# Hybrid attention trunk: the sums of weight blocks kept unit by unit in DRAM and moved as rows of 8 KB, and the last norm's sum and roots taken through TensorE and PSUM

## The chip, the core and the metric

The kernel runs on one core of one Trainium2 chip. The metric is the device time of one execution in microseconds (us); a kernel's figure is the median of its timed runs. A profile is one further execution with the hardware profiler on. Its engines are called PE (TensorE; PEld is its weight load), ACT (ScalarE), DVE (VectorE), POOL (GpSimd) and SP (SyncE, which here only issues DMAs).

## The reference

One layer of a streaming encoder in float32: 2,048 frames of 1,024 features, 16 heads of 64, chunked attention with a learned relative bias, then a SwiGLU block with 2,816 hidden features. Each sub-layer stands between two RMS norms.

```python
def rms_norm(x, g):
    y = x * lax.rsqrt(jnp.mean(x * x, axis=-1, keepdims=True) + RMS_EPS)
    return y * g

def reference(x, ...):
    h = rms_norm(x, g_pre_mix)
    m = chunk_relpos_attention(h, w_qkv, w_o, rel_bias)   # chunk c sees chunks c-8 .. c
    x = x + rms_norm(m, g_post_mix)
    h = rms_norm(x, g_pre_ffn)
    return x + rms_norm((silu(h @ w_gate) * (h @ w_up)) @ w_down, g_post_ffn)
```

## The kernel before, in words

**Layout and products.** Activations lie transposed, features on the 128 partitions and tokens along the free dimension, in blocks of 512 tokens (`HALF`); two blocks make a group, and there are two groups. Every dense product is done with float32 split in two parts (`split`, `split_part`: a rounded part by ACT, the rest by a DVE subtraction, L128/L129 for weights and L347/L348 for activations) and takes three matmuls (`products`, L192 to L194).

**Order of the work.** TensorE's order is written out by hand; the other engines' orders are chosen by the scheduler within the data's dependencies, and each engine then runs its own queue strictly in order. So an instruction that waits holds up all that stands behind it on its engine. Work that belongs beside the matmuls is put in a list (`later`) of steps with a cost; `tick` runs steps as matmuls are emitted, one tick for three matmuls of 512 columns, and `pause(w)` is an empty step of w ticks.

**Attention.** For each group 64 slots are run (16 jobs of a pair of heads, four blocks of 128 queries each). In a slot PE computes the scores (L555/L556), DVE adds the bias and finds the maximum (L564), ACT takes the exponentials and their sums (L568), DVE the reciprocals (L571), POOL scales the probabilities (L572, one per head), and PE transposes them (L588, and the fifth block at L599), from where DVE and ACT copy them to SBUF (L591, L593, L600). The slots are filled up with the dense products of the following jobs.

**The feed-forward block** uses a seven-product scheme for a two-by-two block product (Strassen's, in Winograd's form). Of the factors on the weights' side four are sums of weight blocks, S1 to S4: S1 = A21 + A22, S2 = A11 + S1, S3 = A11 + A21, S4 = A12 + S2, the differences being all on the activations' side. They are made once, beside the attention, for 11 gate/up units (128 x 1024 floats, 512 KB a block) and 11 down units (128 x 512 floats, 256 KB), in DRAM alone: `weight_sums` yields steps, of which one is run per slot (t from 5 to 51 in the first group, 0 to 51 in the second). A step holds DRAM-to-DRAM copies of a first term, issued from SP (`copy`, through the helper at L71), and accumulating DMAs of a second term, issued from POOL (`add`, L868). An add is put behind POOL's last softmax scaling (`issue_after`), so it stands in POOL's queue between the scalings of two slots. Units take turns, gate/up and down; unit u's four copies are in the steps 4u to 4u+3, its adds in 4u+5, 4u+6, 4u+8 and 4u+11. The program reserves 512 bytes of each SBUF partition for the descriptors of such DMAs (`dynamic_dma_scratch_size`). A sum is a tensor of 128 rows with the unit's index inside the row, so a block is moved as 128 pieces of 4 KB or 2 KB; the blocks of the down weights lie the same way. During the feed-forward block the factors are read back, `gate_up_stream` and `down_stream`, through SP.

**The end.** The last group's down product ends with the second half of its output columns for token block 0. That last product is done in two halves of 256 tokens; after each, `ended` puts the norm of that half on the list. `rstd_steps` adds the squares over the partitions by matmuls against a column of ones, one per 128 tokens (L258), takes mean and epsilon on DVE (L260), the power -1/2 on POOL (L262), and `spread` transposes the roots to rows on PE (L274) and copies them to SBUF by ACT (L275). The squares of each output tile are taken by ACT (L243) and added up by DVE (L244); the tile itself comes from PSUM through a DVE addition (L1075). `finish` multiplies the output by the roots (L1375), adds the residual (L1376), both on DVE, two tiles of 128 features a time for the first half and four for the second, and issues the store. The norm of the other token block (`Post.finish`) was done beside the product before; there half of the residual sums run on POOL (L392).

Of the kernel before, what the change touches and what calls it, by code (L numbers as in the profile page):

```python
# [9 lines left out]
F32 = mybir.dt.float32  # L10
F32R = mybir.dt.float32r
AF = mybir.ActivationFunctionType
ALU = mybir.AluOpType
# [3 lines left out]
P = 128  # L17
# [33 lines left out]
def trunk(  # L51
# [162 lines left out]
    def pause(w):  # L214
        return [(w, lambda: None)]
# [27 lines left out]
        act.activation(sq, src, AF.Square)  # L243
        eng.tensor_tensor(total, total, sq, op=ALU.add)  # L244

    def rstd_steps(total, dst, wait=8.0, keep=None, bank=None):

        nb = total.shape[-1] // P
        bank = bank or norm_bank
        r = {}

        def by_token():
            pt = bank("pssq")
            for b in range(nb):
                pe.matmul(pt[:, 0, b : b + 1], total[:, b * P : b * P + P], ones[:, 0:1], start=True, stop=True)  # L258
            m = const.tile([P, 4], F32, tag="ms", name="ms", bufs=2)
            dve.tensor_scalar(m[:, :nb], pt[:, 0, :nb], 1.0 / D, EPS, op0=ALU.mult, op1=ALU.add)  # L260
            r[0] = const.tile([P, 4], F32, tag="rs", name="rs", bufs=2) if keep is None else keep
            pool.tensor_tensor(r[0][:, :nb], m[:, :nb], neg_half.to_broadcast([P, nb]), op=ALU.pow)  # L262

        return [(1.0, by_token)] + pause(wait) + [(1.0, lambda: spread(r[0], dst, bank))]

    def norm_bank(name):
        return ps.tile([P, 4, P], F32, tag="mm", name=name)

    def spread(r, dst, bank=norm_bank):

        pt = bank("prs")
        nb = dst.shape[-1] // P
        for b in range(nb):
            pe.transpose(pt[:, b, :], r[:, b : b + 1].to_broadcast([P, P]), ident)  # L274
        act.activation(dst, pt[:, :nb, :].rearrange("p b t -> p (b t)"), AF.Copy)  # L275

    class Prep:

# [569 lines left out]
    NC = NF // 2  # L848

    def gate_up_at(c):  # L850
        return {n: w_gu[c, BLOCK_AT[n]] for n in BLOCK_AT}, {n: sum_gu[n][:, c, :] for n in sum_gu}

    def down_at(c):
        return {n: w_d[BLOCK_AT[n]][:, c, :] for n in BLOCK_AT}, {n: sum_d[n][:, c, :] for n in sum_d}

    units = [at(c) for c in range(NC) for at in (gate_up_at, down_at)]

    def weight_sums():

        def copy(to, a):
            with tc.issue_after(last_sp[0].ins):
                sp.dma_start(to, a)

        def add(to, a):
            with tc.issue_after(last_pool[0].ins):
                pool.dma_start(to, a, accum_op=ALU.add)  # L868
# [25 lines left out]
    def gate_up_stream(c, n):  # L894

        a = FACTOR[n]

        def load():
            raw = phase["fp"].tile([P, 1024], F32, tag="w4", name="raw4", bufs=4)
            sp.dma_start(raw, w_gu[c, BLOCK_AT[a]] if a in BLOCK_AT else sum_gu[a][:, c, :])  # L900
            return raw

        def make(raw):
            w = w_tile(f"gu{c}_{n}")
            split_part(*w, raw)
            return w

        return load, make, 4, 3

    def down_stream(g, n, c):  # L910

        a = FACTOR[n]

        def load():
            raw, cols = narrow("raw_d"), narrow("raw_a")
            src = w_d[BLOCK_AT[a]] if a in BLOCK_AT else sum_d[a]
            sp.dma_start(raw, src[:, c, :])
# [347 lines left out]
    def dense():  # L1265
# [59 lines left out]
        for g in range(NG):  # L1325
# [29 lines left out]
            total, begun = [], set()  # L1355
# [12 lines left out]
            def finish(here, per):  # L1368

                n = here.stop - here.start  # L1370
                r = total[0][:, here].rearrange("p (o t) -> p o t", o=1).to_broadcast([P, per, n])

                def one(k):
                    a, b_ = (v[:, k : k + per, here] for v in (y[0], res[0]))
                    dve.tensor_tensor(a, a, r, op=ALU.mult)  # L1375
                    dve.tensor_tensor(b_, b_, a, op=ALU.add)  # L1376
                    sp.dma_start(out[i][:, k : k + per, here], b_)

                return [(0.0, lambda k=k: one(k)) for k in range(0, KT, per)]

            def ended(n):
                if n == 0:
                    post = Post([y[1][:, dt, :] for dt in range(KT)], total[1], POST_FFN, res[1], out[i + 1])
                    later.extend(pause(4.0) + rstd_steps(post.total, post.total, 5.0) + post.finish(2.0, 2))
                    return
                drain()
                first, second = slice(0, N), slice(N, HALF)
                here = (first, second)[n - 1]
                later.extend(pause((1.0, 0.0)[n - 1]) + rstd_steps(total[0][:, here], total[0][:, here], 3.0))
                if n == 2:  # L1390
                    later.extend(finish(first, 2) + finish(second, 4))

            yield from down(g, keep, ended)
            drain()
# [100 lines left out]
def _layout(inputs):  # L1495
# [10 lines left out]
    for p in range(NPAIR):  # L1506
# [19 lines left out]
        "w_d": np.stack([wd[:, j::2, HALF * i : HALF * i + HALF] for i, j in ((0, 0), (1, 0), (1, 1), (0, 1))]),  # L1526
    }


# [18 lines left out]
```

## Time and profile before

| | |
|---|---|
| median of 3 runs | 2446.33 us |
| fastest, slowest of them | 2441.12, 2449.23 us |
| the profiled execution, its own time | 2441.91 us |
| its span, first to last instruction | 2440.1 us |
| mean granted TensorE clock | 0.996 of full |
| DMA | 488.41 MB, mean 200 GB/s |
| adds' queue (software) | 12,672 packets, 34.61 MB |

The profile is one execution. Its views are read so: the page gives busy times and shares per engine; the list of waits tells which group of instructions waited for which, with the total, the count and the longest; a timeline row has start, duration, engine, line, operation, tiles, shapes and count, with the idle time ahead of it and what ended that in brackets ("issue" is idle time that the profile explains by no semaphore); a windows row has a stretch, its length, the busy time and count of PE, PEld, DVE, ACT and POOL, the granted clock, the DMA engines' busy share and GB/s. Matmuls are pipelined: one of 512 columns is shown for 0.39 us, but they start 0.23 us apart.

### The profile page before, as it was taken

The page shows a single profiled execution, that of the slowest core. Times are in us where ns is not written, and L with a number is a line of the kernel's source. Part 1 is how long each engine was busy: PE and PEld are TensorE (multiplying, and loading weights), DVE is VectorE, ACT ScalarE, POOL GpSimd, SP SyncE. Part 2 cuts the span into 40 slices and gives each one's busy share as a digit, 9 for nine tenths or more (in the row PEclk, how much of TensorE's full clock was granted, in tenths as well). Part 3 has the DMA queues.
Part 4 walks back from the last instruction along what each step waited for, and adds up shares of the span by engine and source line. Part 5 has one row for each costly group of instructions (what it writes and reads, how often), then busy time and mean ns, then how long its engine had stood idle before and what let it go on. Part 6 is the DMA issues. An engine that isn't in the chain of part 4 may idle for free.

```text
span 2440.1 us, 34891 instructions
## 1 busy us (share of the span) xinstructions
PE 2399.6 (98%) x12554; PEld 1993.0 (82%) x12554; DVE 1468.8 (60%) x2569; ACT 1030.7 (42%) x1807; POOL 302.6 (12%) x379
## 2 busy tenths in 40 slices
PE   9999999999999999999999999999999999999997
PEld 8887878788888888878888788888888888888886
DVE  6555455767555554667566665577666655555577
ACT  5444334654344443545333333365443333334444
POOL 0233233201233332210000000000000000000001
PEclk9999999999999999999999999999999999999999
DMA  7689888757898975546476755377667655457654
GB/s 219 196 216 234 221 229 203 222 183 200 226 250 214 243 182 133 144 143 225 157 252 201 242 171 170 123 246 256 210 214 246 219 178 160 135 170 243 195 188 147
DMA packets 209884, 488.41 MB, mean 200 GB/s; under 512 B 25360, under 2 KB 27424, under 8 KB 208432
## 3 DMA queue, kind: packets, MB, share of 16 engines
q1 hardware_dynamic: 197040, 451.59, 58.3%
q0 software_dynamic: 12672, 34.61, 9.3%
q8 instruction: 99, 1.62, 0.3%
q14 instruction: 73, 0.60, 0.1%
HBM read 356.54 MB, written 148.42 MB: 207 GB/s over the span
## 4 chain that ended last, share of the span: by engine, by line
PE 48%; DMA 4%; DVE 3%; issue 1%; ACT 0%; SPq 0%; DVEq 0%; ACTq 0%
PE pd L192 6%; PE pd L193 6%; PE pd L194 6%; PE pb L192 4%; PE pb L193 4%; PE pb L194 4%; PE pa L192 3%; PE pa L193 3%; PE pa L194 3%; PE pc L192 3%; PE pc L194 3%; PE pc L193 3%; DMA b<-x 1%; DMA res<-in_x 1%; DMA y<-y 1%
## 5 line engine op out<-in xcount | busy, mean ns | idle before, releaser
L568 ACT ACTIVATE sc<-sc,nmax 128x640 f32<-128x640 f32 (+4 forms) x256 | 193.1, 756 | 277.5 <-DVE nmax L564 276.7
L192 PE MATMUL mm<-hb,whi 128*128 128x512 f32 x704 | 290.0, 412 | 0.5 <-ACT y L239 0.5
L194 PE MATMUL mm<-hb,wlo 128*128 128x512 f32 x704 | 277.0, 393 | 0.0
L193 PE MATMUL mm<-hb,whi 128*128 128x512 f32 x704 | 276.1, 392 | 0.0
L572 POOL TENSOR_SCALAR sc<-sc,rows 128x640 f32<-128x640 f32 (+4 forms) x256 | 198.6, 813 | 438.4 <-DVE rows L571 418.7
L564 DVE CUSTOM_DVE_ANT_0 sc<-st,bias 128x640 f32<-128x640 f32 (+4 forms) x256 | 179.6, 738 | 100.2 <-PE st L556 94.9
L192 PE MATMUL pb<-hb,whi_gu_T 128*128 128x512 f32 x528 | 206.9, 392 | 4.8 <-DVE terms L980 4.8
L194 PE MATMUL pb<-hb,wlo_gu_T 128*128 128x512 f32 x528 | 206.0, 390 | 0.0
L193 PE MATMUL pb<-hb,whi_gu_T 128*128 128x512 f32 x528 | 205.9, 390 | 0.0
L262 POOL TENSOR_TENSOR rs<-ms,neg_half 128x4 f32<-128x4 f32 (+1 forms) x11 | 16.7, 1520 | 1248.1 <-DVE ms L260 1248.1
L192 PEld LDWEIGHTS mm<-hb,whi 128*128 128x128 f32 x704 | 132.9, 189 | 35.2 <-issue 14.7
L194 PEld LDWEIGHTS mm<-hb,wlo 128*128 128x128 f32 x704 | 132.4, 188 | 29.4
L193 PEld LDWEIGHTS mm<-hb,whi 128*128 128x128 f32 x704 | 133.1, 189 | 19.4
L193 PE MATMUL pd<-a,whi_d_T 128*128 128x512 f32 (+1 forms) x368 | 139.9, 380 | 0.4 <-DVE a L348 0.4
L192 PE MATMUL pd<-a,whi_d_T 128*128 128x512 f32 (+1 forms) x368 | 140.0, 381 | 0.0
L194 PE MATMUL pd<-a,wlo_d_T 128*128 128x512 f32 (+1 forms) x368 | 139.7, 380 | 0.0
L192 PE MATMUL pa<-hb,whi_gu_B 128*128 128x512 f32 x352 | 137.7, 391 | 0.5 <-ACT terms L961 0.5
L193 PE MATMUL pa<-hb,whi_gu_B 128*128 128x512 f32 x352 | 137.0, 389 | 0.0
L194 PE MATMUL pa<-hb,wlo_gu_B 128*128 128x512 f32 x352 | 137.0, 389 | 0.0
L192 PE MATMUL mm<-whi,hb 128*128 128x256 f32 x448 | 133.5, 298 | 0.0
L555 PE MATMUL st<-k,q 128*128 128x384 f32 (+1 forms) x448 | 131.9, 315 | 0.2 <-DVE nmax L564 0.2
L129 DVE TENSOR_TENSOR wlo_gu_T<-raw,whi_gu_T 128x1024 fp32r<-128x1024 f32 x88 | 107.4, 1221 | 40.5 <-ACT whi_gu_T L128 40.3
(219 smaller groups left out, 5642.8 us busy)
## 6 DMA issues: line engine op xcount, KB each, us to landing
raw<-gu_S SPq DMA_DIRECT2D x88, 512.0 KB, 3.9
raw<-in_w_gu SPq DMA_DIRECT2D x66, 512.0 KB, 4.1
q<-stage SPq DMA_DIRECT2D x128, 256.0 KB, 5.8
y<-y SPq DMA_DIRECT2D x96, 256.0 KB, 3.8
gu_S<-in_w_gu SPq DMA_DIRECT2D x44, 512.0 KB, 7.6
raw_a<-aT SPq DMA_DIRECT2D x88, 256.0 KB, 3.6
raw_d<-d_S SPq DMA_DIRECT2D x88, 256.0 KB, 3.6
raw<-in_w_a SPq DMA_DIRECT2D x42, 512.0 KB, 6.3
```

The lines of the kernel that those rows point to most:

```text
L129: dve.tensor_tensor(lo, raw, hi.bitcast(F32), op=ALU.subtract)
L192: pe.matmul(pt, a_hi, b_hi, start=first, stop=False, skip_group_check=go_on)
L193: pe.matmul(pt, a_hi, b_lo, start=False, stop=False, skip_group_check=go_on)
L194: pe.matmul(pt, a_lo, b_hi, start=False, stop=last, skip_group_check=go_on)
L262: pool.tensor_tensor(r[0][:, :nb], m[:, :nb], neg_half.to_broadcast([P, nb]), op=ALU.pow)
L555: pe.matmul(st[:, a:b], q[:, 2 * h, cols], kk[:, h, key], start=True, stop=False)
L564: dve.tensor_tensor_reduce(out=sc[:, :n], in0=st[:, c0 : c0 + n], in1=rev, scale=-1.0, scalar=3.0e38, op0=ALU.add, op1=ALU.min, accum_out= ...
L568: act.activation(sc[:, :n], sc[:, :n], AF.Exp, bias=nmax, scale=-1.0, accum_out=rows[:, 0:1])
L572: last_pool[0] = pool.tensor_scalar(sc[:, :n], sc[:, :n], rows[:, 1:2], 1.0, op0=ALU.mult, op1=ALU.mult)
```

## The change

Two parts that touch each other nowhere.

*The sums.* Their tensors, and the down weights on the host, are laid out unit by unit, so that one unit's block is contiguous. Copies and adds see a block as 64 longer rows and are limited to 8 KB a row: 64 rows for a gate/up block, 32 for a down block. A pair of units (gate/up c and down c) now shares 8 steps: the four copies of the gate/up unit are in the steps 8c, 8c+2, 8c+4, 8c+6, its adds in 8c+4 (S1), 8c+8 (S2), 8c+10 (S3) and 8c+14 (S4), and the down unit does the same one step later. Each step so has one copy and one add, of a large and a small block by turns.

*The end.* The squares of token block 0's last feature tile stay apart; `rstd_steps` adds them by a second matmul per 128 tokens (`extra`). The roots' rows aren't copied to SBUF: `finish` reads them from PSUM (`then`), and the sums and roots use the banks "pd". `finish` takes two feature tiles a time in both halves; POOL adds the residual for the first two tiles of the first half and for the first four of the second, DVE for the rest, and `finish` of both halves is now one step, `end`. The other block's norm begins after a pause of 6 ticks, not 4.

```diff
-    sum_gu = {n: dram.tile([P, NF // 2, 1024], F32, name=f"gu_{n}") for n in ("S1", "S2", "S3", "S4")}
-    sum_d = {n: dram.tile([P, NF // 2, HALF], F32, name=f"d_{n}") for n in ("S1", "S2", "S3", "S4")}
+    sum_gu = {n: dram.tile([NF // 2, P, 1024], F32, name=f"gu_{n}") for n in ("S1", "S2", "S3", "S4")}
+    sum_d = {n: dram.tile([NF // 2, P, HALF], F32, name=f"d_{n}") for n in ("S1", "S2", "S3", "S4")}
...
             for b in range(nb):
-                pe.matmul(pt[:, 0, b : b + 1], total[:, b * P : b * P + P], ones[:, 0:1], start=True, stop=True)
+                terms = [total] if extra is None else [total, extra]
+                for n, t in enumerate(terms):
+                    pe.matmul(
+                        pt[:, 0, b : b + 1], t[:, b * P : b * P + P], ones[:, 0:1],
+                        start=n == 0, stop=n == len(terms) - 1,
+                    )
...
+        def back():
+            if then is None:
+                spread(r[0], dst, bank)
+            else:
+                then(transposed(r[0], nb, bank))
...
+        def long(t):
+            return t.rearrange("(a b) c -> a (b c)", b=2)
 
         def copy(to, a):
             with tc.issue_after(last_sp[0].ins):
-                sp.dma_start(to, a)
+                last_sp[0] = nc.sync.dma_start(long(to), long(a), max_dma_last_dim=8192)
 
         def add(to, a):
             with tc.issue_after(last_pool[0].ins):
-                pool.dma_start(to, a, accum_op=ALU.add)
+                pool.dma_start(long(to), long(a), accum_op=ALU.add, max_dma_last_dim=8192)
 
         steps = [[] for _ in range(4 * len(units) + 8)]
         for u, (src, dst) in enumerate(units):
+            at = 8 * (u // 2) + u % 2
             for n, (to, a) in enumerate((("S1", "A21"), ("S3", "A11"), ("S2", "A11"), ("S4", "A12"))):
-                steps[4 * u + n].append((copy, dst[to], src[a]))
-            for n, to, a in ((5, "S1", src["A22"]), (6, "S3", src["A21"]), (8, "S2", dst["S1"]), (11, "S4", dst["S2"])):
-                steps[4 * u + n].append((add, dst[to], a))
+                steps[at + 2 * n].append((copy, dst[to], src[a]))
+            for n, to, a in ((2, "S1", src["A22"]), (4, "S2", dst["S1"]), (5, "S3", src["A21"]), (7, "S4", dst["S2"])):
+                steps[at + 2 * n].append((add, dst[to], a))
...
                 put(y[t][:, dt, here])
-                add_square(y[t][:, dt, here], total[t][:, here], t not in begun)
+                if t == 0 and dt == KT - 1:
+
+                    last_sq[here.start] = narrow("sq")[:, : here.stop - here.start]
+                    act.activation(last_sq[here.start], y[t][:, dt, here], AF.Square)
+                else:
+                    add_square(y[t][:, dt, here], total[t][:, here], t not in begun)
...
+                def one(k, eng):
+                    a, b_ = (v[:, k : k + 2, here] for v in (y[0], res[0]))
                     dve.tensor_tensor(a, a, r, op=ALU.mult)
-                    dve.tensor_tensor(b_, b_, a, op=ALU.add)
-                    sp.dma_start(out[i][:, k : k + per, here], b_)
-
-                return [(0.0, lambda k=k: one(k)) for k in range(0, KT, per)]
+                    eng.tensor_tensor(b_, b_, a, op=ALU.add)
+                    sp.dma_start(out[i][:, k : k + 2, here], b_)
+
+                return [lambda k=k: one(k, pool if k < KT - 2 * n else dve) for k in range(0, KT, 2)]
...
-                    later.extend(pause(4.0) + rstd_steps(post.total, post.total, 5.0) + post.finish(2.0, 2))
+                    later.extend(pause(6.0) + rstd_steps(post.total, post.total, 5.0) + post.finish(2.0, 2))
...
+                def end():
+
+                    for step in finish(rows_[0], first, 3):
+                        step()
+                    for step in finish(rows_[1], second, 2):
+                        step()
+
+                later.extend(roots(second, hold(1)) + [(0.0, end)])
```

More of the change, by code (lines that the diff above doesn't have):

```diff
@@ L244, in add_square, with rstd_steps @@
         eng.tensor_tensor(total, total, sq, op=ALU.add)
-    def rstd_steps(total, dst, wait=8.0, keep=None, bank=None):
+    def rstd_steps(total, dst, wait=8.0, keep=None, bank=None, extra=None, then=None):
         nb = total.shape[-1] // P
@@ L262, in by_token @@
             pool.tensor_tensor(r[0][:, :nb], m[:, :nb], neg_half.to_broadcast([P, nb]), op=ALU.pow)
-        return [(1.0, by_token)] + pause(wait) + [(1.0, lambda: spread(r[0], dst, bank))]
+        def back():
[3 more added lines that the diff above has]
+                then(transposed(r[0], nb, bank))
+        return [(1.0, by_token)] + pause(wait) + [(1.0, back)]
     def norm_bank(name):
@@ L1354, in dense @@
             res = [hb_tile((6, 0)[t], F32, (KT, HALF)) for t in range(2)]
-            total, begun = [], set()
+            total, begun, last_sq, rows_ = [], set(), {}, [None, None]
             for t in range(2):
@@ L1366, in keep, with finish, roots @@
                     act.activation(z, z, AF.Copy, scale=gt[:, POST_FFN, dt : dt + 1])
[L1368 to L1376, printed above, removed]
-                    sp.dma_start(out[i][:, k : k + per, here], b_)
-                return [(0.0, lambda k=k: one(k)) for k in range(0, KT, per)]
+            def finish(r, here, n):
+                w = here.stop - here.start
+                r = r.rearrange("p (o t) -> p o t", o=1).to_broadcast([P, 2, w])
+                def one(k, eng):
+                    a, b_ = (v[:, k : k + 2, here] for v in (y[0], res[0]))
+                    dve.tensor_tensor(a, a, r, op=ALU.mult)
+                    eng.tensor_tensor(b_, b_, a, op=ALU.add)
+                    sp.dma_start(out[i][:, k : k + 2, here], b_)
+                return [lambda k=k: one(k, pool if k < KT - 2 * n else dve) for k in range(0, KT, 2)]
+            def roots(here, then):
+                return rstd_steps(
+                    total[0][:, here], None, 3.0, extra=last_sq[here.start], then=then,
+                    bank=lambda name: bank(name).rearrange("p (a b) -> p a b", a=4),
+                )
             def ended(n):
@@ L1387, in ended, with hold @@
                 first, second = slice(0, N), slice(N, HALF)
[L1388 to L1391, printed above, removed]
+                def hold(m):
+                    return lambda r: rows_.__setitem__(m, r)
+                if n == 1:
+                    later.extend(pause(1.0) + roots(first, hold(0)))
+                    return
+                def end():
[4 more added lines that the diff above has]
+                later.extend(roots(second, hold(1)) + [(0.0, end)])
             yield from down(g, keep, ended)
@@ L1524, in _layout @@
         "w_gu": np.stack([np.stack([b.reshape(P, 1024) for b in c]) for c in gu]),
[L1526 removed]
+        "w_d": np.stack([
+            np.transpose(wd[:, j::2, HALF * i : HALF * i + HALF], (1, 0, 2)) for i, j in ((0, 0), (1, 0), (1, 1), (0, 1))
+        ]),
     }
```

14 lines of the change are left out of this document (7 added, 7 removed).

## The prediction

> **What bounds the kernel now.** I read the page first, then who TensorE waited for, then the stretches where it stood still, then the queue behind the longest of these stalls, and last the end of the span.
>
> ```profile
> span 2440.1 us, 34891 instructions
> PE 2399.6 (98%) x12554; PEld 1993.0 (82%) x12554; DVE 1468.8 (60%) x2569; ACT 1030.7 (42%) x1807; POOL 302.6 (12%) x379
> ```
>
> TensorE (PE) is busy 98% of the span, so work taken off another engine is worth nothing in itself. Only the 40.5 us in which PE stands still (2440.1 less 2399.6) and stretches at a lower clock can be won. The waits of PE:
>
> ```profile
> PE tt L588 <- POOL sc L572: 8.2, 3, 4.7
> PE tt L599 <- DVE pT L591: 5.8, 8, 1.5
> PE pb L192 <- DVE terms L980: 4.8, 3, 3.1
> ```
>
> The largest is 8.2 us in three waits for the softmax scaling on GpSimd (POOL), though POOL is busy only 12% of the span. So POOL is not slow there, it is held. Its own order of work round the two long waits, with the division (L571) that releases the scaling:
>
> ```profile
> 239.83 0.85 POOL L868 DMA_DIRECT2D gu_S<-in_w_gu  x1 [5.29 <-DVE t L492]
> 247.44 0.85 POOL L868 DMA_DIRECT2D gu_S<-in_w_gu  x1 [5.15 <-DVE ot L623]
> 255.57 0.84 POOL L868 DMA_DIRECT2D d_S<-d_S  x1 [5.67 <-DVE pT L600]
> 258.95 0.15 DVE L571 RECIPROCAL rows<-rows 128x1 f32<-128x1 f32 x1
> 264.83 0.87 POOL L868 DMA_DIRECT2D gu_S<-gu_S  x1 [6.81 <-issue]
> 265.43 1.11 POOL L572 TENSOR_SCALAR sc<-sc,rows 128x640 f32<-128x640 f32 x1
> 266.59 0.66 PE L588 MATMUL tt<-ident,sc 128*128 128x128 f32 x4 [2.90 <-POOL sc L572]
> 341.08 0.85 POOL L868 DMA_DIRECT2D gu_S<-gu_S  x1 [6.10 <-DVE nmax L564]
> 342.34 0.16 DVE L571 RECIPROCAL rows<-rows 128x1 f32<-128x1 f32 x1 [0.30 <-ACT sc L568]
> 351.36 0.87 POOL L868 DMA_DIRECT2D d_S<-d_S  x1 [8.25 <-issue]
> 351.95 1.66 POOL L572 TENSOR_SCALAR sc<-sc,rows 128x512 f32<-128x512 f32 x2
> ```
>
> The reciprocals of the second tile were there at 342.50, the scaling started at 351.95. Ahead of it in POOL's queue stood an accumulating DMA of the weights' sums (L868), issued at 351.36. What held that one? The landings of the adds issued at 255.57 and at 341.08, each asked for alone, and then the group of all 88:
>
> ```profile
> DMA to landing us min/median/max: 8.9/8.9/8.9
> DMA to landing us min/median/max: 10.0/10.0/10.0
>   issue: 151.0, 49
> DMA to landing us min/median/max: 4.1/6.6/10.5
> ```
>
> 255.57 + 8.9 is 264.5, and the next add starts at 264.83; 341.08 + 10.0 is 351.1, and the next starts at 351.36. So an add starts some 0.3 us after the add before it has landed, though the two write different sums. Of the 87 adds that follow another, 66 start so, and none sooner. One add at a time is in flight; POOL spends 151.0 us in 49 waits that no semaphore explains. What is short must be room for descriptors: two adds of 128 rows never fit. Where an add takes longer to land than a slot of the attention lasts, the next slot's scaling comes late, then PE's transposes.
>
> A long stall costs twice. The clock after these two:
>
> ```profile
> 266.60:271.00 4.40, 4.29 (x25) 4.05 (x26) 0.93 (x2) 0.60 (x1) 0.70 (x1) 0.68 1.05 280
> 352.80:357.50 4.70, 4.49 (x16) 3.68 (x17) 1.45 (x3) 1.11 (x2) 1.57 (x4) 0.64 0.48 85
> ```
>
> The granted clock (third number from the right) is 0.68 and 0.64 in these 4.4 and 4.7 us: 4.4 x 0.32 + 4.7 x 0.36 = 3.1 us of PE work lost.
>
> **Part 1: the sums.** The same bytes are copied and added, 88 copies on SP and 88 adds on POOL. What changes is the rows: 64 of 8 KB for a gate/up block, 32 for a down block, in place of 128; and the order, a gate/up add alternating with a down add. The room that takes 128 rows once takes 64 + 32 = 96, so two neighbours can be in flight if a row needs no more descriptors than before. Then an add waits at most for the one two steps back. A step is a slot of the attention, 7.6 us by the first two adds shown (239.83 to 247.44), so that one was issued some 15 us before, longer than the slowest landing of 10.5. POOL's hold goes, the three waits (8.2) go, and with the two long ones the slow clock (3.1): **11.3 us**. What is late next is the vector copy in front of the second transposes (L599): 5.8 us in eight waits, of which the list for 200 to 400 us alone has
>
> ```profile
> PE tt L599 <- DVE pT L591: 1.9, 2, 1.5
> ```
>
> These may shrink with an earlier scaling, so the part's upper end is 13.2. The lower end is nothing: if the room doesn't count rows, every add still waits.
>
> The trace has no accumulating row of 8 KB. Its price, from the queue of the adds:
>
> ```profile
> q0 software_dynamic: 12672, 34.61, 9.3%
> gu_S<-in_w_gu SPq DMA_DIRECT2D x44, 512.0 KB, 7.6
> ```
>
> 9.3% of 16 engines over 2440.1 us is 3,631 us for 12,672 packets, 0.29 us each. With the bytes unchanged and the rows fewer, the total can stay (all of it per byte) or fall by up to two thirds (all of it per row); an 8 KB row takes at most about four times the mean row (2.7 KB). I take no change: with POOL free nobody on PE's path awaits a landing. The copies, 7.6 us to land, now come four steps (30 us) before their add at the nearest, where it was five; POOL would stand in that wait with the next slot's scaling behind it, but 30 us cover 7.6. The stores' new order in DRAM leaves every later load at the same size; I set it at nothing, as the loads are issued ahead of use and PE has no wait on one.
>
> The Trainium skill bears on both sides of this. Its page "DMA: Bandwidth & Descriptors", section "SWDGE vs HWDGE vs iDMA", says that GpSimd's descriptors are appended to rings in an SBUF carve-out; by that rule halving the rows makes room, which is the 11.3. Its section "SDMA does more than copy" gives 2,048 elements as the most that one inline add takes, so 8 KB of float32 is just one; no run here shows an add's row above 4 KB.
>
> **Part 2: the end.** The chain after PE's last product:
>
> ```profile
> 2426.11 0.42 DVE L1075 TENSOR_TENSOR hb<-pd,hb 128x256 f32<-128x256 f32 x1
> 2426.56 0.42 ACT L243 ACTIVATE sq<-hb 128x256 f32<-128x256 f32 x1 [1.18 <-DVE hb L1075]
> 2427.04 0.42 DVE L244 TENSOR_TENSOR total<-total,sq 128x256 f32<-128x256 f32 x1
> 2427.61 0.58 PE L258 MATMUL pssq<-ones,total 128*128 128x1 f32 x4 [2.08 <-DVE total L244]
> 2428.53 1.07 POOL L262 TENSOR_TENSOR rs<-ms,neg_half 128x2 f32<-128x2 f32 x1 [6.35 <-DVE ms L260]
> 2429.66 0.69 PE L274 MATMUL prs<-ident,rs 128*128 128x128 f32 x2 [1.48 <-POOL rs L262]
> 2430.39 0.38 ACT L275 ACTIVATE total<-prs 128x256 f32<-128x256 f32 x1 [2.87 <-PE prs L274]
> 2430.80 2.36 DVE L1375 TENSOR_TENSOR hb<-hb,total 128x1024 f32<-128x1024 f32 x2
> 2433.08 2.35 DVE L1376 TENSOR_TENSOR hb<-hb,hb 128x1024 f32<-128x1024 f32 x2
> out_dram<-hb SPq DMA_DIRECT2D x2, 512.0 KB, 3.2
> out_dram<-hb SPq DMA_DIRECT2D x4, 256.0 KB, 2.2
> ```
>
> - *L244 leaves the chain*: from the square's end (2426.98) to PE is 0.63, of which a hand-off of 0.15 stays (L244's end to PE): 0.5 won. PE sums a second term instead: four more one-column matmuls, about 0.15 each by the row of four, two of them behind the last square: 0.3 given back. Net 0.2.
> - *The copy L275 leaves it*: PE ends at 2430.35, DVE starts at 2430.80; a hand-off of 0.1 stays. 0.35 won.
> - *Second half's products and sums*: four operations of 1,024 columns end at 2435.43, 4.6 us. Now DVE has four products and two sums of 512 columns, 0.6 each (half of these): 3.6; POOL has two sums. Those it does have a price in the trace, from the norm of the other tile:
>
> ```profile
> 2385.50 5.35 POOL L392 TENSOR_TENSOR hb<-hb,hb 128x512 f32<-128x512 f32 x1 [5.02 <-DVE hb L389]
> 2390.81 1.28 POOL L392 TENSOR_TENSOR hb<-hb,hb 128x512 f32<-128x512 f32 x1
> ```
>
>   The same sum took 1.28 us where DVE read PSUM or was idle and 5.35 us where DVE ran one SBUF operation after the other. At best POOL ends with DVE (3.6, 1.0 won); at worst it gets nothing until DVE is through and then needs 2 x 1.28: 6.2, 1.6 lost. The products now read the roots from PSUM, so I lean to the free row and take 4.2: 0.4 won.
> - *The last transfer* is 256 KB, not 512: 2.2 for 3.2, 1.0 won.
>
> The end together: **2.0 us**, between 0 and 2.6. One wait is new: the first half's POOL sum can stand in POOL's queue ahead of the second half's roots (L262). Begun at about 2425, as early as the first half's products allow (an estimate), and stretched to 5.35, it ends 1.8 us after 2428.53, and everything behind it, the two transposes, DVE and the stores, moves by that: lower end -1.8.
>
> The skill's page "SBUF — State Buffer", section "Who interferes with whom", speaks against moving these sums: a vector instruction with both inputs in SBUF and a GpSimd instruction that reads SBUF block each other for a whole instruction. The two rows agree. By it the products are harmless and only DVE's own sums block; the end comes 0.6 us later for each of them that does.
>
> Smaller: the first half's sum of squares puts four more tiny matmuls (0.6 by L258's row) in PE's stream but no longer waits for L244: 0.2 lost. The other tile's norm comes two ticks later:
>
> ```profile
> 2364.94 1.05 PE L258 MATMUL pssq<-ones,total 128*128 128x1 f32 x8 [0.83 <-DVE total L244]
> ```
>
> Two ticks are six matmuls, about 1.4 us, more than the 0.83 that PE waits: 0.8 won; its own chain still has the 61 us from there to 2426 as cover.
>
> **Sum.** 11.3 + 2.0 - 0.2 + 0.8 = 13.9 us. The profiled execution took 2441.91 (span 2440.1 and 1.8 around it) and would take 2428.0. It lies 4.4 below the median of the three runs, 2446.33; I carry the difference over to the median: **2432.4 us**. What this kernel's measurement can tell from no change is about 0.3%, 7.3 us: faster means below 2439.0.
>
> **Rivals.**
> - *Adds still one at a time* (0.17). For it: the 0.3 us after a landing is all the trace knows; no two adds were ever in flight, so the limit may be one DMA, or an 8 KB row may take two descriptors. Then part 1 brings nothing and 2.6 remain: 2443.7, no change.
> - *The stall moves* (0.15). DMA reads 1.05 of its engines in one of the stretches above, and PE, 11 us earlier, meets the vector copies (5.8 us, L599) and half of the waits in other places: 5.6 + 2.6 won, 2438.1, at the edge of faster.
> - *Slower* (0.09): long accumulating rows hold up the loads that share the engines. A row of 8 KB at 0.29 us per 2.7 KB takes 0.87 instead of 0.43 for 4 KB; a load of four rows behind four such rows lands 1.7 us later. With one add a slot, 21 of them in the 160 us up to 360, that costs 21 x 1.7 = 36 us if every load were due on the spot: 2446.3 + 36 - 13.9 = 2468; it decides only where a load has less than 1.7 us to spare. Against it: PE has no wait on a weight there.
>
> **How the numbers follow.** My forecast has 0.59, at 2432.4; its own bounds are 13.2 + 2.6 - 0.2 + 0.8 = 16.4 at best (2425.5 from the profiled execution's own time) and, with the end at -1.8 and only the two long waits gone, some 5 us less than the sum. The range 2423 to 2446 takes in the second and third case and leaves out the slower one and a twentieth below. Faster: 0.59 and over half of the third case, 0.68. Same: 0.23. Slower: 0.09.
>
> **What would show it.** Right: adds that start before the last one lands; the wait of L588 on L572 gone and the clock at 1.00 from 260 to 360 us; the idle time "issue" before L868 near nothing; L244 and L275 absent between the last square and the last product; the last transfer 2.2 us. Wrong: adds still 0.3 us behind a landing, new PE waits on weights between 200 and 400, a POOL sum of over 3 us ahead of L262, or the 3.1 us wait on L980 in several places.

## The result, and the profile after

The changed kernel took 2425.65 us (median of 6 runs, 2421.82 to 2429.38) beside 2445.10 (6 runs, 2441.12 to 2454.10): ratio 0.9916, 95% interval 0.9895 to 0.9937. Run once more, it took 2426.87 (6 runs) beside 2441.06 (14 runs): 0.9939, 0.9920 to 0.9958. Over the two the gain is some 14 to 19 us; the forecast of 2432.4 was a ratio of 0.9943. The profiled execution took 2425.50 us, 16.4 less than that of before.

The page, and the list of whom TensorE (PE) waited for:

```profile
span 2423.7 us, 34890 instructions
PE 2394.3 (99%) x12562; PEld 1991.3 (82%) x12562; DVE 1462.4 (60%) x2568; ACT 1029.7 (42%) x1805; POOL 294.0 (12%) x382
```

```profile
PE pb L192 <- DVE terms L998: 4.6, 4, 1.9
PE tt L613 <- DVE pT L605: 2.9, 4, 1.8
PE po L631 <- DVE pT L605: 2.6, 1, 2.6
```

One line of the list before, for the last of these (L617 then):

```profile
PE po L617 <- DVE pT L591: 0.8, 1, 0.8
```

The transposes' 8.2 us of waits for the softmax scaling (now L586) are gone from the list altogether. Those for the vector copy (L613, L599 before) halved, and the one wait of the product at L631 grew from 0.8 to 2.65 us. GpSimd's own order of work, where before it stood in front of an add (L868, now L886):

```profile
241.16 1.61 POOL L586 TENSOR_SCALAR sc<-sc,rows 128x640 f32<-128x640 f32 x2 [3.05 <-DVE rows L585]
242.71 0.78 POOL L886 DMA_DIRECT2D d_S<-d_S  x1
249.32 1.60 POOL L586 TENSOR_SCALAR sc<-sc,rows 128x640 f32<-128x640 f32 x2 [5.84 <-DVE rows L585]
250.86 0.80 POOL L886 DMA_DIRECT2D gu_S<-gu_S  x1
255.35 1.69 POOL L586 TENSOR_SCALAR sc<-sc,rows 128x640 f32<-128x640 f32 x2 [3.69 <-DVE rows L585]
256.98 0.78 POOL L886 DMA_DIRECT2D d_S<-d_S  x1
260.19 0.74 POOL L586 TENSOR_SCALAR sc<-sc,rows 128x128 f32<-128x128 f32 x2 [2.43 <-DVE rows L585]
```

No add here has idle time in brackets: each follows the scaling at once, and what GpSimd waits for in these rows is the reciprocal alone. Of the 87 adds that follow another, 38 start before the one ahead has landed (none before the change), and 4 start 0.2 to 0.4 us behind a landing (66 before). The stretch from 200 to 360 us, before and after (length, then busy time and count of PE, PEld, DVE, ACT and POOL, the granted clock, DMA share, GB/s):

```profile
200.00:360.00 160.00, 149.52 (x899) 122.90 (x898) 80.38 (x203) 60.15 (x138) 48.27 (x66) 0.98 0.90 238
```

```profile
200.00:360.00 160.00, 160.00 (x1015) 134.01 (x1014) 86.46 (x227) 66.84 (x153) 50.20 (x72) 1.00 0.95 251
```

PE doesn't stand still in it at all, at full clock. How far that carries is read from the same two score products in both traces, before first:

```profile
238.11 0.41 PE L555 MATMUL st<-k,q 128*128 128x384 f32 x1 [0.21 <-DVE nmax L564]
358.46 0.33 PE L555 MATMUL st<-k,q 128*128 128x384 f32 x1
```

```profile
236.88 0.34 PE L569 MATMUL st<-k,q 128*128 128x384 f32 x1
342.04 0.33 PE L569 MATMUL st<-k,q 128*128 128x384 f32 x1
```

The kernel was 1.2 us ahead at the first and is 16.4 ahead at the second: 15.2 us won between them. It is 14.7 ahead when PE begins its last product and 16.4 at the end of the span. So the sums' part carries nearly all, a little of it is given back on the way, and the end brings 1.75. The end's rows, to be laid beside the prediction's:

```profile
2411.14 0.42 DVE L1093 TENSOR_TENSOR hb<-pd,hb 128x256 f32<-128x256 f32 x1
2411.59 0.42 ACT L1383 ACTIVATE sq<-hb 128x256 f32<-128x256 f32 x1 [0.90 <-DVE hb L1093]
2412.52 0.36 PE L261 MATMUL pssq<-ones,sq 128*128 128x1 f32 x2
2413.23 1.08 POOL L268 TENSOR_TENSOR rs<-ms,neg_half 128x2 f32<-128x2 f32 x1 [1.48 <-DVE ms L266]
2414.37 0.43 PE L288 MATMUL prs<-ident,rs 128*128 128x128 f32 x2 [1.49 <-POOL rs L268]
2414.84 0.69 DVE L1399 TENSOR_TENSOR hb<-hb,prs 128x512 f32<-128x512 f32 x1 [0.49 <-PE prs L288]
2415.45 0.68 DVE L1400 TENSOR_TENSOR hb<-hb,hb 128x512 f32<-128x512 f32 x1
2416.05 1.88 DVE L1399 TENSOR_TENSOR hb<-hb,prs 128x512 f32<-128x512 f32 x3
2417.84 1.79 DVE L1400 TENSOR_TENSOR hb<-hb,hb 128x512 f32<-128x512 f32 x2
2415.61 2.88 POOL L1400 TENSOR_TENSOR hb<-hb,hb 128x512 f32<-128x512 f32 x2 [1.29 <-DVE hb L1399]
```

From the add of the last output row to the first product it was 4.69 us (2426.11 to 2430.80) and is 3.70. VectorE's (DVE's) addition and copy are out of the chain, and the two transposes take 0.43 in place of 0.69. From the start of PE's last product to the end of the span the tail was 14.88 us and is 13.13. This length varies little (13.12 to 13.38 us in the three profiles with the changed end, 14.54 to 14.89 in the seven with the old one), so the end is judged by it, or from the last row's add: 12.58 us in the changed kernel.

### The profile page after: what moved, and what is told of

It reads as the page before. It is cut to its first block, busy times and chain, and to the rows that moved or that the text cites. A ratio compares the mean times of both kernels' runs of the same rounds, so it can differ in the third digit from the quotient of the medians.

```text
span 2423.7 us, 34890 instructions
## 1 busy us (share of the span) xinstructions
PE 2394.3 (99%) x12562; PEld 1991.3 (82%) x12562; DVE 1462.4 (60%) x2568; ACT 1029.7 (42%) x1805; POOL 294.0 (12%) x382
## 3 DMA queue, kind: packets, MB, share of 16 engines
q0 software_dynamic: 5632, 34.61, 8.7%
## 4 chain that ended last, share of the span: by engine, by line
PE 52%; DMA 3%; DVE 2%; issue 0%; ACT 0%; SPq 0%; POOL 0%; DVEq 0%; ACTq 0%
PE pd L193 6%; PE pd L192 6%; PE pd L194 6%; PE pb L192 4%; PE pb L193 4%; PE pb L194 4%; PE pa L192 3%; PE pa L193 3%; PE pa L194 3%; PE pc L192 3%; PE pc L193 3%; PE pc L194 3%; PE mm L192 1%; PE mm L194 1%; PE mm L193 1%; DMA y<-y 1%
## 5 line engine op out<-in xcount | busy, mean ns | idle before, releaser
L586 POOL TENSOR_SCALAR sc<-sc,rows 128x640 f32<-128x640 f32 (+4 forms) x256 | 192.0, 752 | 654.7 <-DVE rows L585 616.0
L192 PEld LDWEIGHTS mm<-hb,whi 128*128 128x128 f32 x704 | 132.5, 188 | 35.1 <-issue 14.7
```

Source lines behind the costliest of these rows:

```text
L192: pe.matmul(pt, a_hi, b_hi, start=first, stop=False, skip_group_check=go_on)
L586: last_pool[0] = pool.tensor_scalar(sc[:, :n], sc[:, :n], rows[:, 1:2], 1.0, op0=ALU.mult, op1=ALU.mult)
```

## The experiments

Theory: descriptor room was short for two adds, so GpSimd stood in its queue until one had landed; fewer rows make room. Rivals: it is the order or the layout, or the long rows themselves. For the end: two operations less on the chain, a shorter last transfer, and GpSimd's sums, whose worth was open.

**Each part alone.** The sums' part without the end, and the end without the sums' part.

```diff
 # the sums' part alone: L97-98, L851-875, L900-917, "w_d" as in the change; rstd_steps, finish, ended as before
 # the end alone: rstd_steps, spread, transposed, finish, ended as in the change; weight_sums and layouts as before
```

> The kernel before with the first part alone (new layout, rows of 8 KB, new steps). Room theory (an add of 128 rows leaves no descriptor room for a second; with 64 and 32 rows two and more fit): adds start before the one ahead has landed, the three waits of L588 on POOL go, the clock stays at 1.00 between 260 and 360 us, and the run is 11 to 17 us faster than before (ratio 0.993 to 0.9955). If the end part carries a good deal of the gain, this run is less than 8 us faster.

> The kernel before with the second part alone (squares summed by PE, roots read from PSUM, POOL sums, longer pause). By my steps 2.6 us faster, ratio 0.999, which a measurement can't tell from no change; from the last pd matmul to the end of the span 1 to 2 us less than before. The waits of L588 on POOL stay as before (about 8 us). If the end carries more than I think, 5 us or more.

The sums' part: 2431.42 us beside 2443.26, ratio 0.9947 (0.9928 to 0.9966), no wait on the scaling. The end alone: 2442.17, 0.9994 (0.9981 to 1.0007), which time alone can't tell from nothing; its tail is 13.12 us, as in the changed kernel (sums' part alone: 14.86), so its gain is there in the trace. The wait that it leaves in place, and that even grew in this profile:

```profile
PE tt L602 <- POOL sc L586: 11.5, 5, 3.6
```

**Room alone.** The kernel before, nothing changed but the bytes reserved for descriptors.

```diff
-    nc = bacc.Bacc("TRN2", ..., dynamic_dma_scratch_size=512)
+    nc = bacc.Bacc("TRN2", ..., dynamic_dma_scratch_size=640)
```

> The kernel before with 640 bytes of descriptor room in place of 512, nothing else: rows, layout and steps stay. Room theory: if an add of 128 rows takes a little over half of the 512 bytes, two fit now; adds start before the one ahead has landed, and most of the sums' gain is there, 8 to 17 us (ratio 0.993 to 0.997). Rival, the rows themselves (fewer and longer pieces make an add shorter for POOL or on the DMA engines): adds still start 0.31 us after a landing, no gain (ratio 0.998 to 1.002). If adds still start only after a landing, it can also be that 640 is still too little.

2432.84 us, ratio 0.9943 (0.9917 to 0.9969): the whole gain of the sums' part, with 128 rows of 4 or 2 KB. Its stretch:

```profile
200.00:360.00 160.00, 159.20 (x1005) 132.91 (x1004) 85.89 (x224) 66.14 (x150) 52.29 (x73) 1.00 0.96 258
```

One add of 87 starts 0.2 to 0.4 us behind a landing, 37 before it. So room was the cause, and long rows are only one way to get it.

**Layout and steps, without the long rows.**

```diff
-                last_sp[0] = nc.sync.dma_start(long(to), long(a), max_dma_last_dim=8192)
+                last_sp[0] = nc.sync.dma_start(to, a, max_dma_last_dim=4 * to.shape[-1])
-                pool.dma_start(long(to), long(a), accum_op=ALU.add, max_dma_last_dim=8192)
+                pool.dma_start(to, a, accum_op=ALU.add, max_dma_last_dim=4 * to.shape[-1])
```

> The first part alone, but its copies and adds moved as 128 rows of 4 KB or 2 KB as before; the new layout and the new steps with large and small blocks by turns stay. Room theory: an add of 128 rows fills the room again, adds start 0.31 us after a landing, the 8 us of waits of L588 on POOL are back, no gain over before (ratio 0.998 to 1.002). Rival, the new order or the contiguous blocks do it: 8 to 17 us faster as with the long rows.

2446.44 us, ratio 1.0008 (0.9993 to 1.0023), 61 adds behind a landing, and the waits are back:

```profile
PE tt L588 <- POOL sc L572: 8.3, 7, 2.6
```

```profile
200.00:360.00 160.00, 151.25 (x909) 121.73 (x909) 78.40 (x203) 60.30 (x138) 47.74 (x66) 0.99 0.90 236
```

**Long rows, with the room taken away.**

```diff
-    nc = bacc.Bacc("TRN2", ..., dynamic_dma_scratch_size=512)
+    nc = bacc.Bacc("TRN2", ..., dynamic_dma_scratch_size=192)
```

> The sums' part alone (rows of 8 KB, large and small by turns, the end as before), with 192 bytes of descriptor room in place of 512. Room theory: two adds of 128 rows did not go together in 512 bytes and did in 640, so one takes between 256 and 320 bytes and an add of 64 rows about 128 to 160; 192 bytes hold one and not two. Then some 60 of 87 adds start 0.31 us after the landing before them, the products' waits on GpSimd's scaling are back with 8 us or more, and the time is that of the kernel before, 2440 to 2447 us (ratio 0.998 to 1.002). Rival (it is the few long rows, their turns or their landings that keep GpSimd free): nothing changes with the room, no wait on GpSimd, 2431 us (ratio 0.995).

2443.76 us, ratio 0.9991 (0.9970 to 1.0011), 59 adds behind a landing:

```profile
PE tt L588 <- POOL sc L572: 6.2, 8, 2.5
```

```profile
200.00:360.00 160.00, 154.15 (x930) 124.13 (x929) 83.39 (x211) 62.75 (x143) 48.01 (x67) 0.99 0.88 235
```

The room theory was met but for the size of the waits (6.2 us where 8 or more were expected): from 200 to 360 us the adds land in 6.8 us by the median, 7.2 in the kernel before, which would hold GpSimd for less; that was not tried by itself. One pair of adds did overlap with 192 bytes, two of 32 rows (166 to 175 us). With this and the two before, room is shown from both sides.

**Long rows, old steps.**

```diff
-                steps[at + 2 * n].append((copy, dst[to], src[a]))
+                steps[4 * u + n].append((copy, dst[to], src[a]))
-            for n, to, a in ((2, "S1", ...), (4, "S2", ...), (5, "S3", ...), (7, "S4", ...)):
-                steps[at + 2 * n].append((add, dst[to], a))
+            for n, to, a in ((5, "S1", ...), (6, "S3", ...), (8, "S2", ...), (11, "S4", ...)):
+                steps[4 * u + n].append((add, dst[to], a))
```

> The sums' part alone with the step numbers of the kernel before (large and small not by turns), rows of 8 KB kept, the end as before. Room theory: two neighbours fit whatever their order, no wait on GpSimd's scaling, 2429 to 2434 us (ratio 0.993 to 0.996). Rival (the turns matter, since large neighbours ask for GpSimd again before the first has landed): 20 or more adds start 0.31 us after a landing, 3 us or more of the waits on GpSimd are back, 2436 to 2441 us.

2433.01 us, ratio 0.9950 (0.9929 to 0.9970), no add behind a landing.

```profile
200.00:360.00 160.00, 160.00 (x1016) 134.00 (x1015) 87.17 (x227) 66.79 (x153) 50.55 (x72) 1.00 0.96 252
```

The turns of large and small bring nothing; two large neighbours fit as well.

**Do the two parts add up?** The medians of the first runs lie 5.8 us apart (2431.42 and 2425.65), more than the tail's 1.75 and the 0.8 of the other block's norm. The sums' part alone and the changed kernel were run again on one chip, unchanged (so there is no diff).

> The changed kernel once more, beside the sums' part alone on the same chip. Theory (the two parts add up; the 5.8 us between the medians of the first runs hold 3 us of stalls on splits of the activations near 780, 1365 and 1380 us, which come and go from run to run): the median lies 2 to 4 us under the sums' part alone, and the stretches at half clock of its profile stand elsewhere than the one at 445.5 us. Rival (the parts help one another, or this program's placement is free of these stalls): 5 us or more under the sums' part alone again, and the same single stretch near 445 us.

> The sums' part alone once more. Theory: 2 to 4 us above the changed kernel, stretches at half clock not where the first profile had them (781.6 and 1365.3 us). Rival: 5 us or more above the changed kernel, the same stretches.

2426.87 and 2429.29 us (ratios 0.9939 and 0.9952): 2.4 apart, as the theory has it. The stretches at half clock moved too. The changed kernel had one at 445.5 us and now has one at 1364.1; the sums' part alone had them at 781.6 and 1365.3 and now has one at 445.5. They follow waits that a run has in one place or another.

**The end, taken apart.** Four edits of the changed kernel, one profile each; the time can't tell them apart, the tail can. *The roots copied to SBUF:*

```diff
-                    return lambda r: rows_.__setitem__(m, r)
+                    def go(r):
+                        to = total[0][:, (first, second)[m]]
+                        act.activation(to, r, AF.Copy)
+                        rows_[m] = to
+                    return go
```

> The changed kernel with one edit: the transposed roots are copied from PSUM to SBUF by ScalarE, and VectorE's products read the SBUF copy, as in the kernel before. Judged by the tail, from the start of the last product of the down projection to the end of the span: 13.13 us in the changed kernel, 14.88 before. Theory (the copy stands on the chain, 0.35 us and two hand-offs, and this is why the first product came 1.3 us sooner where 0.55 was worked out): 13.6 to 13.9 us. Rival (the copy costs its 0.35 us or is hidden, and the gain came from elsewhere): 13.1 to 13.4 us; a product from SBUF may also be blocked by GpSimd's sums, and then the sums of the first half take longer.

The tail is 16.29 us, 3.16 more than in the changed kernel. Neither expectation has that, though the second named the blocking. 1.38 of it lies ahead of the last row's add. The copy of the first half's roots delays VectorE's products there by 0.31, and one of these products, with both inputs in SBUF, runs beside GpSimd's sum of the first half and takes 1.75 us where it is 0.68. The last row's add stands behind it in VectorE's queue:

```profile
2408.45 1.32 POOL L1400 TENSOR_TENSOR hb<-hb,hb 128x512 f32<-128x512 f32 x1 [3.30 <-issue]
```

```profile
2408.57 1.75 DVE L1399 TENSOR_TENSOR hb<-hb,total 128x512 f32<-128x512 f32 x1
2410.25 0.41 DVE L1093 TENSOR_TENSOR hb<-pd,hb 128x256 f32<-128x256 f32 x1
```

From the last row's add to the end it is 14.36 us, where it is 12.58: the other 1.78. The second half's copy, products and GpSimd's sums:

```profile
2414.20 0.38 ACT L1422 ACTIVATE total<-prs 128x256 f32<-128x256 f32 x1 [2.55 <-PE prs L288]
```

```profile
2414.62 0.69 DVE L1399 TENSOR_TENSOR hb<-hb,total 128x512 f32<-128x512 f32 x1 [1.16 <-ACT total L1422]
2415.23 0.68 DVE L1400 TENSOR_TENSOR hb<-hb,hb 128x512 f32<-128x512 f32 x1
2415.83 4.02 DVE L1399 TENSOR_TENSOR hb<-hb,total 128x512 f32<-128x512 f32 x3
2419.77 1.28 DVE L1400 TENSOR_TENSOR hb<-hb,hb 128x512 f32<-128x512 f32 x2
```

```profile
2415.39 1.64 POOL L1400 TENSOR_TENSOR hb<-hb,hb 128x512 f32<-128x512 f32 x1 [1.97 <-DVE hb L1399]
2417.72 1.58 POOL L1400 TENSOR_TENSOR hb<-hb,hb 128x512 f32<-128x512 f32 x1 [0.69 <-DVE hb L1399]
```

The copy costs 0.41 on the chain and the slower transposes 0.26 (0.69 for 0.43; they fall into the lower clock, as in the second run of the changed kernel). The larger part is elsewhere: three products with both inputs in SBUF take 4.02 us where three that read the roots from PSUM take 1.88. GpSimd's sum runs to 2417.03 and the product begun at 2415.83 ends at 2417.58, 0.55 later; DVE stood until GpSimd was through. From the first product to the last sum it is 6.43 in place of 4.79, 1.64 more, and the stores give 0.53 back (2.34 from the last sum to its landing, for 2.87): 0.41 + 0.26 + 1.64 - 0.53 = 1.78. The two copies so cost 0.31 and 0.41, the held products 1.07 and 1.64: reading PSUM is worth more for what it leaves free than for the copies that it saves.

*All sums on DVE:*

```diff
-  lambda k=k: one(k, pool if k < KT - 2 * n else dve)
+  lambda k=k: one(k, dve)
```

> The changed kernel with all row sums of the last stage on VectorE, none on GpSimd. Tail in the changed kernel 13.13 us. Theory (GpSimd carries three sums beside VectorE, which at 0.67 us each for VectorE would lengthen its phase): VectorE's phase from the first product to the last sum is 4.8 us and gets 2 sums more in the second half, 1.3 to 1.4 us, and part of the first half's sum: tail 14.3 to 14.8 us. Rival (what GpSimd adds is paid back in sums that stretch beside it, as one did to 1.19 us): 13.1 to 13.6 us.

Tail 13.93 us: between the two. GpSimd's sums win 0.8, not 1.2 to 1.7. DVE ends 1.33 us later behind the last row's add (9.82 for 8.49), as the theory has it, but its stores come spread out and the last one again takes 2.34 to land.

*The last square added by DVE again, no extra term:*

```diff
-                if t == 0 and dt == KT - 1:
+                if False:
-                    ..., extra=last_sq[here.start], then=then,
+                    ..., then=then,
```

> The changed kernel with the last square added by VectorE's operation of 0.41 us again, and no extra term for TensorE. From the start of VectorE's add of the last output row to the end: 12.58 us in the changed kernel. The account that the prediction gave (0.41 us leave the chain, two matmuls of 0.11 us come): 12.8 us. Rival (a hand-off and VectorE's queue went with it, as the 0.58 us won up to the last matmul of the squares' sum say): 13.1 to 13.3 us.

13.32 us from the last row's add, 0.74 more than the changed kernel. That is at the rival's upper end, but 0.26 of it is the clock; without that it is 13.06, between the two. 0.48 lies between the add and the end of the squares' sum (2.23 for 1.75): DVE's addition with its hand-offs, which also waits behind a row sum in DVE's queue. 0.26 is the two transposes, which here fall into the lower clock:

```profile
2419.41 0.69 PE L288 MATMUL prs<-ident,rs 128*128 128x128 f32 x2 [1.49 <-POOL rs L268]
```

*GpSimd adds twice in the first half:*

```diff
-                    for step in finish(rows_[0], first, 3):
+                    for step in finish(rows_[0], first, 2):
```

> The changed kernel with two of the first half's row sums on GpSimd in place of one. Judged from the start of VectorE's add of the last output row to the end of the span: 12.58 us in the changed kernel. Theory (a sum of the first half, 0.68 us, that is left over in VectorE's queue behind the second half's first product goes): 11.9 to 12.1 us, and the median of the runs at most 1 us lower, which the measurement can't tell. Rival (the second sum of GpSimd, 1.3 to 1.7 us, ends after 2413.2 us, where the root's operation is waiting behind it in GpSimd's queue): 12.5 to 13.2 us.

12.59 us, nothing won, and not by the rival's mechanism. GpSimd was through at 2411.59, before the roots' operation could start (2411.84). DVE's queue:

```profile
2411.60 0.16 DVE L266 TENSOR_SCALAR ms<-pssq 128x2 f32<-128x2 f32 x1 [0.85 <-POOL hb L1400]
2411.68 0.68 DVE L1400 TENSOR_TENSOR hb<-hb,hb 128x512 f32<-128x512 f32 x1
2412.28 0.68 DVE L1399 TENSOR_TENSOR hb<-hb,prs 128x512 f32<-128x512 f32 x1
2413.45 0.69 DVE L1399 TENSOR_TENSOR hb<-hb,prs 128x512 f32<-128x512 f32 x1 [0.49 <-PE prs L288]
2414.05 0.69 DVE L1400 TENSOR_TENSOR hb<-hb,hb 128x512 f32<-128x512 f32 x1
```

The place of the sum taken away became 0.85 us of waiting, since the mean (L266) stands ahead of the rest in the queue. The last sum of the first half is still run between the second half's products. The order put there by the scheduler decides, not the amount of work. Its median, 2426.32 us, is that of the changed kernel; no version here beats it measurably.

## Why the prediction was right

- *What bounds: right.* GpSimd was held, not slow, by room for descriptors. That GpSimd's descriptors lie in rings in an SBUF carve-out, as the Trainium skill's "DMA: Bandwidth & Descriptors" has it in the section "SWDGE vs HWDGE vs iDMA", agrees with the run of 640 bytes. The adds' packets are the rows plus 16 of 4 bytes an add (88 x 128 + 88 x 16 = 12,672 before). The same page's 2,048 elements an add ("SDMA does more than copy") agrees as well: 44 x 64 + 44 x 32 + 88 x 16 is the 5,632 below, so a row of 8 KB went as one.

```profile
q0 software_dynamic: 5632, 34.61, 8.7%
```

- *The price of long rows: right.* 8.7% of 16 engines over 2423.7 us is 3,374 us, 0.60 us a packet where it was 0.29. The total fell by 7% only; it goes by bytes.
- *Part 1, 11.3 us: too small; 15.2 measured.* The mechanism was right. The three waits were the 8.2 of the sum, but PE stood still for 10.5 us of the stretch from 200 to 360 (160.00 - 149.52), and all of it went: the 1.9 of the vector copies too, which I had put in the upper end alone, and 0.3 in short waits. The slow clock was 3.4 us, not 3.1: two stretches of 3.41 us at half clock, each losing 1.7. That makes 13.9. Most of the last 1.3 I can only argue: a matmul is shown for 0.39 us but the next starts 0.23 later, so each of the seven waits in that stretch hides 0.16 of standing in the time counted as busy, 1.1 together.
- *What is late next.* From 442.8 us PE waits 2.65 us, and the clock halves behind it:

```profile
445.50:448.90 3.40, 3.40 (x10) 2.19 (x12) 1.79 (x6) 1.84 (x5) 2.42 (x4) 0.51 0.40 167
```

```profile
442.44 1.06 ACT L128 ACTIVATE whi<-raw 128x1024 fp32r<-128x1024 f32 x1 [5.40 <-DMA raw<-in_w_o]
```

  The split of a 1 MB weight load stands ahead of the exponentials in ACT's queue, and the load took 9.1 us to land (4.9 the median of its six). The wait was there before the change (0.8 us at 462, that load 7.3), and in runs without the sums' gain: 2.43 with the end alone (load 8.9), 3.06 with rows of 128 (9.5). In the ten profiles with the gain it is 0.5 to 2.7, and on the whole longer the longer the load takes. So it isn't shown that the change brings it; what makes the load late was not tried. The second rival (the stall moves) took half of the 11.3 for lost, and no run shows that.
- *The end, 2.0 us: about right (1.75), by other terms.* The chain up to the first product won 1.30, not 0.55. The last row's add starts 0.31 sooner: the product ahead of it in DVE's queue no longer waits for the copy of the first half's roots, which the prediction left out (with the copy back, the 0.31 were back). From that add on the squares' sum ends 0.33 sooner (net 0.2 was worked out), the copy and its hand-off bring 0.41, and the transposes 0.26, because the clock fell just behind them. That last part is luck: in the second run of the changed kernel the tail is 13.38. Products and sums lost 0.16 (4.63 to 4.79) where 0.4 was to be won: a sum of the first half stands among them, and one of DVE's took 1.19 us beside GpSimd's:

```profile
L1400 DVE TENSOR_TENSOR hb<-hb,hb x5: 677/684/1190, 2411.5 to 2419.0; 128x512 f32<-128x512 f32 x5
L1400 POOL TENSOR_TENSOR hb<-hb,hb x3: 1262/1331/1651, 2410.4 to 2417.2; 128x512 f32<-128x512 f32 x3
```

  The last transfer won 0.49, not 1.0: smaller, but with several stores in flight at once it took 2.87 us, against 3.36 before and 2.2 worked out. The other 0.12 lies behind the last landing. The new wait that was feared did not come: GpSimd was through with its sum of the first half at 2411.75, and the roots' operation starts at 2413.23.
- *GpSimd's price: right.* 1.26 to 1.65 us, near the free row. The rule of the Trainium skill's "SBUF — State Buffer", section "Who interferes with whom", agrees. Three of DVE's sums met GpSimd's: one was held for 0.15 us (0.83 for 0.68), one for 0.51 (1.19), where the estimate had 0.6 for each, and at the third GpSimd was the one held (1.65 for 1.26). The run with the roots in SBUF shows what it takes when the products obey it too.
- *The other rivals* fell: two adds are in flight, and no load group became slow: the weights of the attention's products (512 KB) land in 6.4 us, 6.3 before. One single load did, the second of `in_w_o`, issued at 364 us: 10.7 us in place of 6.2. In the ten profiles with rows of 8 KB it took 9.7 to 14.2, in the four with rows of 4 and 2 KB 5.5 to 6.2. Whether the long rows hold it up, as the third rival has it, was not tried; PE waits for nothing between 360 and 400 us in the changed kernel.
- *The wait of 0.83* at the other block's norm went as worked out; the 0.2 for four tiny matmuls was not measured by itself.
- *The total.* The two profiled executions lie 16.4 us apart, to the digit the prediction's best case. That is luck: its parts are 15.2 and 1.75 less 0.55 given back between them, where the best case had 13.2, 2.6 and 0.6, and the second profile of the changed kernel is 14.5 below that of before.

## What to carry to other kernels

An engine that is busy 12% can bound a kernel through its queue: compare the start of its instructions with the landing of the DMA before, and a constant 0.3 us tells that something other than data is awaited. Try the reserved room alone first; it is one number, and here it gave what new layouts gave. And let VectorE read an operand from PSUM where GpSimd works beside it.

## What the runs showed of the hardware

- In the 14 profiles, start and end aside, each of PE's 18 single waits of 2.58 us or more was followed by 3.41 or 6.83 us at half clock, five of the eight from 2.12 to 2.51, and none of the shorter ones. Two such stretches (504 us with room of 192, 1262 us with rows of 128) followed no wait of that length. So a wait of 2.6 us costs 4.3 or more.
- What decides at the shorter waits can be worked out from the same traces. All changes of the clock in one trace lie whole multiples of 3.413 us apart (in the one before 3.41, 81.92, 3.41, 1020.59 and so on: 1, 24, 1 and 299 times). Divide the span into windows on that grid, and take those at full clock: in each of the 23 windows in which PE stood still for 1.89 us or more, the next one ran at half clock; of the three from 1.79 to 1.85 one did; of the some 9,800 with less only one (before 504 us with room of 192). So it is not the length of a wait but how much of it falls into one window, and where the grid lies differs from run to run.
- The Trainium skill's "TensorE: Matmul & The Clock Gate", section "What's actually happening", has windows of about 3.4 us that run freely; the length of the stretches and the grid agree. Its section "HAM oscillation — how this bites in real kernels" warns of idle gaps over about 3.4 us; here 2.6 were enough in every case, and the measurement decides.
- Accumulating DMA from DRAM to DRAM: 0.33 us per 4 KB packet before the change and 0.63 per 8 KB after it (medians); the landing of an add hardly moved (median 6.6 us before, 6.7 after).
- Room: 512 bytes hold two adds of 64 rows but not two of 128; 640 hold two of 128; 192 hold two of 32 but not one of 64 and one of 32.
